# Retention outputs: a DVE block transposition and 128-byte stores in place of TensorE transposes, with the gate and the norm weight multiplied in the last stage

## The chip, the cores and the metric

One core of one Trainium2 chip runs the whole program, in one launch. The metric is the device time of that launch in microseconds. A core has TensorE (PE in the profile), VectorE (DVE), ScalarE (ACT), GpSimd (POOL), and SyncE (SP), which here issues nearly all transfers; 16 DMA engines move the data.

## What is computed

One layer of a hybrid decoder for 1024 prompt tokens and 8 x 4 sample tokens (1056 columns, NT). The part that matters is the output of the retention branch, four heads of width 512:

```python
def retention_out(o, rg, gn_w):
    mu = jnp.mean(o, axis=-1, keepdims=True)
    var = jnp.mean(jnp.square(o - mu), axis=-1, keepdims=True)
    on = ((o - mu) * lax.rsqrt(var + EPS)).reshape(b, s, RET_VW).astype(rg.dtype)
    return on * gn_w * jax.nn.silu(rg)
...
h_ret = retention_out(ret_o, rg, ret_gn_w) @ w_down_ret
h_mla = (mla_o * jax.nn.silu(mg)) @ w_down_mla
merged = jax.nn.sigmoid(ga) * h_ret + jax.nn.sigmoid(gb) * h_mla
x = x + merged @ w_out
```

Retention itself goes in chunks of 128 tokens: masked scores q k times v within the chunk, q times the state S for what came before, and S = decay x S + (decayed k) v at the end.

## The kernel before

Every fp32 product is made of three matmuls over operands split into a high and a low part (`mac`, `gemm`; names end in h and l, so vnh and vnl are the values' parts, smh and sml the scores', knh and knl the keys', Sth and Stl the state's, qch and qcl the queries'). The high part is a cast, mostly on ACT or POOL, the low part a subtraction on DVE (`lo_of`, L199).

The work runs in stages: projections woven with attention over the sample's cached pages; retention, head after head; MLA attention of the prompt; then the last stage, which multiplies by w_down_mla (eight products, M), by w_down_ret (two halves of eight), by w_out, and adds the embedding term.

The order of instructions on each engine is not the order of the code alone. Stages are generators that yield costs; `woven` interleaves several of them by these costs, and a scheduler with priorities then fixes each engine's queue. Each engine works through its queue in order, and SP does too: a transfer that waits holds up those behind it.

One head of retention is `prompt_chunks`. `front(c)` computes scores (ac<-q,k), transposes k through PSUM (tr<-k) and splits both; `values_of` projects the values of the next chunk (mm<-wv,x: 24 matmuls, spread through the chunk as filler); `back(c)` makes the output po of the chunk (vn x sm, then St x qc), the two halves m = 0, 1 of the state update (vn x kn into PSUM, then S on DVE, its parts Sth on POOL and Stl on DVE), and calls `group_norm`: BATCH_NORM_STATS, a few small steps on DVE and POOL, and on ACT the normalised rows on, 128 tokens x 512.

The last stage needs these outputs with channels on partitions. `gate_out` does that: four TensorE transposes of 128x128 into PSUM (L866), four DVE products with the norm weight gnw and the SiLU gate (L868), which `gate_in` loaded into g before the chunk (L860), and one store of 256 KB to goD (L870). It is called for 8 chunks and once for the 32 sample rows of each head: 36 calls. Those of the sample rows of heads 0 to 2 are put off (list `late`) into the next head's first chunk. Between two heads `sample_state` updates the sample's states (products vst x kx, stored to out_ret_sample) while the next head's q, k and values are projected (mm<-x,w).

In the last stage `gated` loads a 128 x 1056 tile of goD (gl), `split_gated` splits it into gh and gl, and `gate` loads the merge gates. The pool w4 has three slots.

Of the kernel before, what the change touches and what calls it, by code (L numbers as in the profile page):

```python
# [9 lines left out]
F32 = mybir.dt.float32  # L10
# [4 lines left out]
ALU = mybir.AluOpType  # L15
# [4 lines left out]
P = 128  # L20
D = 1024
SEQ = 1024
NB = 8
NS = 4
NR = NB * NS
NT = SEQ + NR
# [4 lines left out]
HR = 4  # L31
DK = 256
DV = 512
# [128 lines left out]
def decode_step(ctx: ExitStack, tc: tile.TileContext, A: dict, O: dict):  # L162
    nc = tc.nc
    pe, act, dve, pool, sp = nc.tensor, nc.scalar, nc.vector, nc.gpsimd, nc.sync
# [3 lines left out]
    dram = ctx.enter_context(tc.tile_pool(name="scratch", bufs=1, space=DRAM))  # L168
# [23 lines left out]
    def b32(ap):  # L192
        return ap.bitcast(F32)
# [4 lines left out]
    def lo_of(out, src, hi):  # L198
        dve.tensor_tensor(out=out, in0=src, in1=b32(hi), op=ALU.subtract)  # L199
# [16 lines left out]
    gaD = [dram.tile([P, NT], F32, tag=f"ga{f}", name=f"ga{f}") for f in range(8)]  # L216
    gbD = [dram.tile([P, NT], F32, tag=f"gb{f}", name=f"gb{f}") for f in range(8)]
    mgD = [dram.tile([P, NT], F32, tag=f"mg{f}", name=f"mg{f}") for f in range(8)]
    gtD, goD = ([dram.tile([P, 4, NT], F32, tag=f"{n}{h}", name=f"{n}{h}") for h in range(HR)] for n in ("gt", "go"))
    latD = dram.tile([P, 5, SEQ], F32, tag="latD", name="latD")  # L220
    xTD = dram.tile([P, 8, NT], F32, tag="xTD", name="xTD")
    pTD = dram.tile([P, 2, NT], F32, tag="pTD", name="pTD")
# [558 lines left out]
    p4 = ph.enter_context(tc.tile_pool(name="p4", bufs=1))  # L781
# [11 lines left out]
    late = []  # L793
# [61 lines left out]
        act.activation(on[:n], po, AF.Identity, bias=nb[:n], scale=s[:n])  # L855
        return on

    def gate_in(h, n, cols):
        g = p4.tile([P, 4, P], F32, tag="g", name="g", bufs=3)[:, :, :n]
        sp.dma_start(g, gtD[h][:, :, cols])  # L860
        return g

    def gate_out(h, on, n, cols, g):
        pt = tr()
        for f in range(4):
            pe.transpose(pt[:, f * P:f * P + n], on[:n, f * P:(f + 1) * P], ident[:n, :n])  # L866
        for f in range(4):
            dve.scalar_tensor_tensor(out=g[:, f, :], in0=pt[:, f * P:f * P + n], scalar=gnw[:, 4 * h + f:4 * h + f + 1],  # L868
                                     in1=g[:, f, :], op0=ALU.mult, op1=ALU.mult)
        sp.dma_start(goD[h][:, :, cols], g)  # L870

    def pair(name, w, bufs, rows_=P):
        return tuple(p4.tile([rows_, w], F32R, tag=name + s, name=name + s, bufs=bufs) for s in "hl")

    def prompt_chunks(h, X):
        q, k = X["q"], X["k"]
        V = {}
        gC = float(np.exp(P * lg[h]))
        S = p4.tile([P, 2 * DV], F32, tag="S", name="S", bufs=1)
        T = {}  # L880
        kd = C("kd", h, 1)

        def front(c):

            sl = slice(c * P, (c + 1) * P)
            pss = ac()
            for m in range(2):
                pe.matmul(pss[:, :P], k[m][:, sl], q[m][:, sl], start=m == 0, stop=m == 1)
            smh, sml = pair("sm", P, 2)
            sm = p4.tile([P, P], F32, tag="smr", name="smr", bufs=1)  # L890
            dve.tensor_tensor(out=sm, in0=pss[:, :P], in1=C("maskT", h, P), op=ALU.mult)
            act.copy(smh, sm)
            lo_of(sml, sm, smh)
            pt = tr()
            for m in range(2):
                pe.transpose(pt[:, m * P:(m + 1) * P], k[m][:, sl], ident)
            kh, kl = pair("kn", DK, 2)
            act.activation(kh, pt[:, :DK], AF.Copy, scale=kd)
            dve.scalar_tensor_tensor(out=kl, in0=pt[:, :DK], scalar=kd, in1=b32(kh), op0=ALU.mult, op1=ALU.subtract)
            return smh, sml, kh, kl  # L900

        def back(c, parts):
            sl = slice(c * P, (c + 1) * P)
            smh, sml, kh, kl = parts
            vh, vl = V.pop(c)
            if c:
                qh, ql = pair("qc", DK, 1)
                for m in range(2):
                    ms = slice(m * P, (m + 1) * P)
                    hi_pool(qh[:, ms], q[m][:, sl])  # L910
                    lo_of(ql[:, ms], q[m][:, sl], qh[:, ms])
            g = gate_in(h, P, sl)
            po = ac()
            mac(po, (smh, sml), (vh, vl), True, c == 0)
            yield 0.65
            for m in range(2 if c else 0):
                Sh, Sl = T["S"]
                ms, vs = slice(m * P, (m + 1) * P), slice(m * DV, (m + 1) * DV)
                mac(po, (qh[:, ms], ql[:, ms]), (Sh[:, vs], Sl[:, vs]), False, m == 1)
                yield 0.65  # L920
            for m in range(2):
                ms, vs = slice(m * P, (m + 1) * P), slice(m * DV, (m + 1) * DV)
                pS = ac()
                mac(pS, (kh[:, ms], kl[:, ms]), (vh, vl), True, True)
                if c:
                    dve.scalar_tensor_tensor(out=S[:, vs], in0=S[:, vs], scalar=gC, in1=pS, op0=ALU.mult, op1=ALU.add)
                else:
                    act.copy(S[:, vs], pS)
                yield 0.65
            if c < 7:  # L930
                Sh, Sl = T["S"] = tuple(p4.tile([P, 2 * DV], F32R, tag="st", name=f"St{n}", bufs=4) for n in "hl")
                for m in range(2):
                    vs = slice(m * DV, (m + 1) * DV)
                    hi_pool(Sh[:, vs], S[:, vs])
                    lo_of(Sl[:, vs], S[:, vs], Sh[:, vs])
            on = group_norm(po, P, C("qd", h, 1), C("qd2", h, 1))
            yield None
            gate_out(h, on, P, sl, g)
            yield 0.43

        def ahead(u):

            for cost in u:
                if cost is None:
                    return
                yield cost

        parts = front(0)
        yield 1.0
        yield from values_of(0, X, V)  # L950
        while late:
            gate_out(*late.pop())
        due = iter(())
        for c in range(8):
            if c == 7:
                X["st"] = [states(h, 0, 0)]
            u = back(c, parts)
            if c < 7:
                parts = front(c + 1)
                yield 1.0  # L960
                yield from woven((chain(due, ahead(u)), 3.9), (values_of(c + 1, X, V), 5.5))
                due = u
        yield None
        yield from due
# [14 lines left out]
    def sample_state(h, X):  # L979
# [3 lines left out]
        sl = slice(SEQ, NT)  # L983
# [3 lines left out]
        pt = tr()  # L987
# [25 lines left out]
        pt = tr()  # L1013
# [10 lines left out]
            dve.tensor_scalar(kxs[i], kt, C("seq2", i, 1), None, op0=ALU.mult)  # L1024
        yield 1.0
        px = ac()
        g = gate_in(h, NR, sl)
# [27 lines left out]
        on = group_norm(po[:NR], NR, C("qdS", h, 1, NR), C("qd2S", h, 1, NR))  # L1055
        yield 1.0
        if h + 1 < HR:
            late.append((h, on, NR, sl, g))
        else:
            gate_out(h, on, NR, sl, g)  # L1060
            yield 0.5

    def head_in(h, X):
        return woven((head_qk(h, X), 42.3), (head_w(h, X), 8.0))
# [26 lines left out]
    ot = slots(mph.enter_context(tc.tile_pool(name="mla", bufs=1, side="right")), "ot", HM)  # L1091
# [12 lines left out]
    def split(raw, hi, lo):  # L1104
        act.copy(hi, raw)
        lo_of(lo, raw, hi)
        return hi, lo
# [286 lines left out]
    xs_, w4 = slots(pz, "x", 23), slots(pz, "w4", 3)  # L1394
    hi_by[0] = act.copy

    def gated(f, pl):
        lo = pl("gl")
        sp.dma_start(b32(lo), goD[f // 4][:, f % 4, :])
        return lo  # L1400

    def split_gated(hi, lo):

        for j in range(3):
            sl = slice(j * TH, (j + 1) * TH)
            split(b32(lo)[:, sl], hi[:, sl], lo[:, sl])
        return hi, lo

    def load_gated(f, pl):
        lo = gated(f, pl)  # L1410
        return split_gated(pl("gh"), lo)

    def gate(src, f):
        t = w4("gate", dt=F32)
# [26 lines left out]
    gx[7] = split_gated(xr_("gh"), gx[7])  # L1441
    merged, nxt = [], []
    for half in range(2):
        for f in range(8):
# [17 lines left out]
        gx = nxt  # L1462
# [18 lines left out]
    for f in range(8):  # L1481
# [3 lines left out]
        hi, lo = xr_("x1h"), xr_("x1l")  # L1485
# [130 lines left out]
```

## Time and profile before

| | |
|---|---|
| median of 3 runs | 2175.15 us (2174.05 to 2175.59) |
| profiled execution | 2167.49 us |
| span of the profiled execution | 2165.7 us |
| TensorE busy | 2125.3 us, 98% |
| DVE / ACT / POOL busy | 1249.4 / 726.9 / 326.4 us |
| granted TensorE clock, mean | 0.998 |
| retention | about 745 to 1358 us of the span |
| w_down_mla, w_down_ret | about 1661 to 1754, 1754 to 1941 us |

The profiled execution is one run; it lies 7.7 us below the median of the others. A row of a timeline names the start, the duration, the engine, the line, and what is written from what. Matmuls overlap in the pipeline, so the time that one takes from TensorE is read from start to start. L numbers of this profile are those of the kernel before; in the changed kernel the lines of the retention stage have other numbers.

### The profile page before, as it was taken

To read this page: it belongs to the slowest core of one execution; us is meant where nothing else is said; L and a number is where in the kernel's file an instruction comes from. 1 tells how busy PE (TensorE), PEld (TensorE's weight loads), DVE (VectorE), ACT (ScalarE), POOL (GpSimd) and SP (SyncE) were. 2 spreads that over 40 slices of the span, in tenths; PEclk is the share of its full clock that TensorE was granted. 3 is DMA by queue.
4 is the path that set the end of the run, shared out by engine and by line. 5 is a ranking of instruction groups with operands and counts; after the bars stand their busy time and mean duration, and the time that the engine had idled before them with its cause. 6 is when DMAs were issued, how large, how long until landed. Compare 5 with 4: busy or idle time off the path is not lost.

```text
span 2165.7 us, 38482 instructions
## 1 busy us (share of the span) xinstructions
PE 2125.3 (98%) x15314; PEld 1854.5 (86%) x15314; DVE 1249.4 (58%) x2799; ACT 726.9 (34%) x1535; POOL 326.4 (15%) x519
## 2 busy tenths in 40 slices
PE   8999999999999999999999999899998999999998
PEld 7988777777777898888888787788888999999998
DVE  5524565565655447666666764777777353444465
ACT  6412222433423322222222211454556342222243
POOL 2210111111100022222222220122221000000022
PEclk9999999999999999999999999999999999999999
DMA  8557666566565321533613517110112453234243
GB/s 231 147 160 256 226 208 232 186 250 231 194 237 181 109 59 49 184 111 94 204 45 119 176 54 260 44 37 12 38 56 72 141 186 99 88 91 125 78 143 117
DMA packets 264356, 299.71 MB, mean 138 GB/s; under 512 B 26544, under 2 KB 221744, under 8 KB 260080
## 3 DMA queue, kind: packets, MB, share of 16 engines
q1 hardware_dynamic: 254960, 213.36, 31.8%
q0 software_dynamic: 9216, 83.89, 10.3%
q8 instruction: 120, 1.97, 0.4%
q14 instruction: 60, 0.49, 0.1%
HBM read 233.03 MB, written 64.17 MB: 137 GB/s over the span
## 4 chain that ended last, share of the span: by engine, by line
PE 41%; DVE 4%; issue 3%; DMA 1%; POOL 1%; ACT 1%; ACTq 0%; POOLq 0%; DVEq 0%
PE mm L266 10%; PE mm L267 10%; PE mm L268 10%; PE mm L1315 2%; PE ac L266 1%; PE ac L267 1%; PE ac L268 1%; PE tr L1301 1%; DMA out_ret_sample_dram<-st 1%; PE ac L1258 1%; PE ac L1259 1%; PE ac L1260 1%; PE ac L1262 1%; PE ac L1261 1%; ACT pr L1276 1%
## 5 line engine op out<-in xcount | busy, mean ns | idle before, releaser
L266 PE MATMUL mm<-xh,wh 128*128 128x352 f32 x1344 | 456.4, 340 | 0.8 <-ACT wh L247 0.6
L267 PE MATMUL mm<-xl,wh 128*128 128x352 f32 x1344 | 435.7, 324 | 0.0
L268 PE MATMUL mm<-xh,wl 128*128 128x352 f32 x1344 | 435.1, 324 | 0.1
L266 PEld LDWEIGHTS mm<-xh,wh 128*128 128x128 f32 x1344 | 252.7, 188 | 91.5 <-issue 78.9
L267 PEld LDWEIGHTS mm<-xl,wh 128*128 128x128 f32 x1344 | 253.9, 189 | 3.3 <-issue 1.0
L268 PEld LDWEIGHTS mm<-xh,wl 128*128 128x128 f32 x1344 | 253.6, 189 | 1.1 <-issue 0.6
L199 DVE TENSOR_TENSOR wl<-wr,wh 128x512 fp32r<-128x512 f32 (+2 forms) x251 | 175.0, 709 | 131.4 <-ACT wh L247 108.0
L247 ACT CAST wh<-wr 128x512 fp32r<-128x512 f32 x216 | 129.7, 618 | 303.3 <-PE mm L267 221.9
L662 DVE STREAM_TRANSPOSE kt<-craw 128x512 f32<-128x512 f32 x256 | 160.8, 681 | 84.4 <-PE sc L666 80.1
L421 ACT ACTIVATE gev<-mm 128x352 f32<-128x352 f32 x120 | 55.5, 463 | 239.3 <-PE mm L268 149.5
L268 PE MATMUL mm<-gh,wl 128*128 128x352 f32 x384 | 124.3, 324 | 0.0
L268 PE MATMUL mm<-mh,wl 128*128 128x352 f32 x384 | 124.3, 324 | 0.0
L266 PE MATMUL mm<-mh,wh 128*128 128x352 f32 x384 | 124.3, 324 | 0.0
L266 PE MATMUL mm<-gh,wh 128*128 128x352 f32 x384 | 124.3, 324 | 0.0
L267 PE MATMUL mm<-ml,wh 128*128 128x352 f32 x384 | 124.2, 324 | 0.0
L267 PE MATMUL mm<-gl,wh 128*128 128x352 f32 x384 | 124.1, 323 | 0.0
L266 PE MATMUL mm<-wv,xh 128*128 128x512 f32 x256 | 103.0, 402 | 0.0
L855 ACT ACTIVATE on<-ac,gb,gs 128x512 f32<-128x512 f32 (+1 forms) x36 | 28.0, 777 | 218.1 <-DVE gb L853 218.0
L267 PE MATMUL mm<-wv,xh 128*128 128x512 f32 x256 | 100.9, 394 | 0.0
L268 PE MATMUL mm<-wv,xl 128*128 128x512 f32 x256 | 100.7, 393 | 0.0
L666 PE MATMUL sc<-kt,q 32*32 32x512 f32 x2560 | 94.8, 600 | 0.1
L1546 POOL TENSOR_TENSOR xr<-x1h,x1l 128x352 f32<-128x352 f32 x24 | 27.0, 1146 | 389.4 <-DVE pT L199 311.1
(389 smaller groups left out, 4563.6 us busy)
## 6 DMA issues: line engine op xcount, KB each, us to landing
wr<-in_w_in_dram SPq DMA_DIRECT2D x144, 256.0 KB, 3.0
st<-in_state_ret_dram SPq DMA_DIRECT2D x32, 512.0 KB, 4.4
out_ret_sample_dram<-st SPq DMA_DIRECT2D x32, 512.0 KB, 4.0
wr<-in_w_ple_gate_dram SPq DMA_DIRECT2D x48, 256.0 KB, 2.8
gt<-gev SPq DMA_DIRECT2D x48, 176.0 KB, 3.5
gl<-go SPq DMA_DIRECT2D x16, 528.0 KB, 5.2
gate<-ga SPq DMA_DIRECT2D x16, 528.0 KB, 3.5
g<-gt SPq DMA_DIRECT2D x32, 256.0 KB, 3.1
```

The costliest lines, as they stand in the source:

```text
L199: dve.tensor_tensor(out=out, in0=src, in1=b32(hi), op=ALU.subtract)
L247: hi_by[0](hi, raw)
L266: pe.matmul(out, wh, xh, start=first, stop=False)
L267: pe.matmul(out, wh, xl, start=False, stop=False)
L268: pe.matmul(out, wl, xh, start=False, stop=last)
L421: act.activation(t, ps, func)
L662: dve.transpose(kt[:, 2 * i + s].rearrange("p (n r) -> p n r", r=32), src)
L666: pe.matmul(sc[32 * v:32 * v + 32, q, :], Q["q4"][qs_, j + v // 2, 2 * (g % 2) + v % 2, :], kt[qs_, v, :], start=n == 0, stop=n == NJ // 2 ...
L855: act.activation(on[:n], po, AF.Identity, bias=nb[:n], scale=s[:n])
L1258: pe.matmul(o, qh[:, qs], kh[:, ks], start=True, stop=False)
L1315: pe.matmul(po[:, :256], v[a][w], t[:, x, 256 * a:256 * a + 256], start=j + a + part == 0, stop=False, skip_group_check=True)
L1546: pool.tensor_tensor(out=xr, in0=b32(x1[f][0][:, sl]), in1=b32(x1[f][1][:, sl]), op=ALU.add)
```

## The change

`gate_in` and `gate_out` go. `turn_out` takes their place: one DVE instruction transposes each 32x32 block of on in place (L861 of the changed kernel, ot<-on), and four stores of 32 partitions each (L863) put the blocks where they belong: each store has 512 pieces of 32 tokens, 128 bytes, 64 KB in all. goD becomes 16 blocks x 32 channels x tokens per head. The gate and the norm weight are now multiplied in the last stage: `gated` loads gt too, into a slot of w4, and `split_gated` multiplies before it splits (three products of 128x352 for each of 16 tiles). Two yields, of 0.43 after a chunk's output and 0.5 after the last head's sample rows, go too, and with them the weaving shifts.

In numbers: 144 TensorE transposes, 144 DVE products of 128x128, 36 loads and 36 stores go; 36 DVE transpositions, 132 stores, 16 loads of 528 KB and 48 DVE products of 128x352 come.

```diff
-    gtD, goD = ([dram.tile([P, 4, NT], F32, tag=f"{n}{h}", name=f"{n}{h}") for h in range(HR)] for n in ("gt", "go"))
+    gtD = [dram.tile([P, 4, NT], F32, tag=f"gt{h}", name=f"gt{h}") for h in range(HR)]
+    goD = [dram.tile([DV // 32, 32, NT], F32, tag=f"go{h}", name=f"go{h}") for h in range(HR)]
...
-    def gate_in(h, n, cols):
...
-    def gate_out(h, on, n, cols, g):
...
+    def turn_out(h, on, n, t0):
+        st = p4.tile([P, DV // 32, 32], F32, tag="g", name="ot", bufs=3)
+        dve.transpose(st[:n], on[:n].rearrange("p (b r) -> p b r", r=32))
+        for a in range(0, n, 32):
+            sp.dma_start(goD[h][:, :, t0 + a:t0 + a + 32].rearrange("b i t -> i b t"), st[a:a + 32])
...
             on = group_norm(po, P, C("qd", h, 1), C("qd2", h, 1))
             yield None
-            gate_out(h, on, P, sl, g)
-            yield 0.43
+            turn_out(h, on, P, c * P)
...
         if h + 1 < HR:
-            late.append((h, on, NR, sl, g))
+            late.append((h, on, NR, SEQ))
         else:
-            gate_out(h, on, NR, sl, g)
-            yield 0.5
+            turn_out(h, on, NR, SEQ)
...
     def gated(f, pl):
         lo = pl("gl")
-        sp.dma_start(b32(lo), goD[f // 4][:, f % 4, :])
-        return lo
+        sp.dma_start(b32(lo), goD[f // 4][4 * (f % 4):4 * (f % 4) + 4].rearrange("b i t -> (b i) t"))
+        gt = w4("gt", dt=F32)
+        sp.dma_start(gt, gtD[f // 4][:, f % 4, :])
+        return f, lo, gt
...
-            split(b32(lo)[:, sl], hi[:, sl], lo[:, sl])
+            dve.scalar_tensor_tensor(out=gt[:, sl], in0=b32(lo)[:, sl], scalar=gnw[:, f:f + 1], in1=gt[:, sl], op0=ALU.mult, op1=ALU.mult)
+            split(gt[:, sl], hi[:, sl], lo[:, sl])
```

DVE's queue in one chunk of a head's middle, from the state update of m = 0 on, before:

```order
L926 SCALAR_TENSOR_TENSOR S<-S,ac 128x512
L851 TENSOR_TENSOR gs<-gr,cst 128x1
L853 SCALAR_TENSOR_TENSOR gb<-mv,gs 128x1
L199 TENSOR_TENSOR Stl<-S,Sth 128x512
L926 SCALAR_TENSOR_TENSOR S<-S,ac 128x512
L891 TENSOR_TENSOR smr<-ac,cst 128x128
L199 TENSOR_TENSOR vnl<-mm,vnh 128x512
L199 TENSOR_TENSOR Stl<-S,Sth 128x512
L199 TENSOR_TENSOR sml<-smr,smh 128x128
L899 SCALAR_TENSOR_TENSOR knl<-tr,cst,knh 128x256
L868 SCALAR_TENSOR_TENSOR g<-tr,gnw,g 128x128 x4
```

and in the changed kernel:

```order
L918 SCALAR_TENSOR_TENSOR S<-S,ac 128x512
L852 TENSOR_TENSOR gs<-gr,cst 128x1
L854 SCALAR_TENSOR_TENSOR gb<-mv,gs 128x1
L199 TENSOR_TENSOR Stl<-S,Sth 128x512
L861 STREAM_TRANSPOSE ot<-on 128x512
L918 SCALAR_TENSOR_TENSOR S<-S,ac 128x512
L199 TENSOR_TENSOR Stl<-S,Sth 128x512
L199 TENSOR_TENSOR vnl<-mm,vnh 128x512
L884 TENSOR_TENSOR smr<-ac,cst 128x128
L892 SCALAR_TENSOR_TENSOR knl<-tr,cst,knh 128x256
L199 TENSOR_TENSOR sml<-smr,smh 128x128
```

The products g stood at the chunk's end; the transposition stands in the middle, ahead of the update and split of the state's second half, and vnl and smr, which stood ahead of the second Stl, now stand behind it.

TensorE's queue at the same place, from the scores of the next chunk on, before:

```order
L888 MATMUL ac<-q_8114,k_8350 128x128
L888 MATMUL ac<-q_8115,k_8351 128x128
L896 MATMUL tr<-cst,k_8350 128x128
L896 MATMUL tr<-cst,k_8351 128x128
L866 MATMUL tr<-cst,on 128x128 x4
L266 MATMUL mm<-wv,xh_113 128x512
L267 MATMUL mm<-wv,xh_113 128x512
L268 MATMUL mm<-wv,xl_114 128x512
L266 MATMUL ac<-vnh,smh 128x512
L267 MATMUL ac<-vnl,smh 128x512
L268 MATMUL ac<-vnh,sml 128x512
```

and in the changed kernel:

```order
L881 MATMUL ac<-q_8114,k_8350 128x128
L881 MATMUL ac<-q_8115,k_8351 128x128
L889 MATMUL tr<-cst,k_8350 128x128
L889 MATMUL tr<-cst,k_8351 128x128
L267 MATMUL ac<-vnh,smh 128x512
L267 MATMUL mm<-wv,xh_113 128x512
L268 MATMUL mm<-wv,xh_113 128x512
L269 MATMUL mm<-wv,xl_114 128x512
L267 MATMUL mm<-wv,xh_115 128x512
L268 MATMUL mm<-wv,xh_115 128x512
L268 MATMUL ac<-vnl,smh 128x512
L269 MATMUL ac<-vnh,sml 128x512
```

With the transposes of on gone, vnh x smh stands right behind the transposes of k, and vnl x smh follows after five value products; before, four transposes and three value products stood ahead of vnh x smh, and vnl x smh came right after it.

TensorE's queue between two heads, around the turning of the sample's values (tr<-vs), before:

```order
L267 MATMUL mm<-xl_120,wh 128x352
L268 MATMUL mm<-xh_119,wl 128x352
L268 MATMUL mm<-xh_113,wl 128x352
L1014 MATMUL tr<-vs,turn 128x512
L266 MATMUL mm<-xh_121,wh 128x352
L267 MATMUL mm<-xl_122,wh 128x352
L266 MATMUL mm<-xh_115,wh 128x352
```

and in the changed kernel, from the sample values' last products (few) on:

```order
L994 MATMUL ac<-wv,few 64x512 x4
L1000 MATMUL tr<-qS,ks_9409 64x32 x2
L1025 MATMUL ac<-st,qm 32x512
L1005 MATMUL tr<-vs,turn 128x512
L1025 MATMUL ac<-st,qm 32x512 x7
L1032 MATMUL ac<-vst,kx 128x512 x2
L267 MATMUL mm<-xh_113,wh 128x352
L268 MATMUL mm<-xl_114,wh 128x352
L267 MATMUL mm<-xh_113,wh 128x352
L268 MATMUL mm<-xl_114,wh 128x352
```

The sample's steps now follow each other with the products st x qm between them; before, the next head's projections (mm<-x,w) lay between.

SP's queue between the first two heads, from the first weights of the next head behind the prompt's last state on, before:

```order
L246 DMA wr<-in_w_in_dram 128x512
L246 DMA wr<-in_w_in_dram 128x4x128 x2
L246 DMA wr<-in_w_in_dram 128x512 x2
L246 DMA wr<-in_w_in_dram 128x4x128 x2
L1046 DMA out_ret_sample_dram<-st 128x2x512 x2
L246 DMA wr<-in_w_in_dram 128x512
L975 DMA st<-in_state_ret_dram 128x2x512 x2
```

and in the changed kernel:

```order
L247 DMA wr<-in_w_in_dram 128x512
L247 DMA wr<-in_w_in_dram 128x4x128 x2
L247 DMA wr<-in_w_in_dram 128x512
L1036 DMA out_ret_sample_dram<-st 128x2x512
L247 DMA wr<-in_w_in_dram 128x512
L1036 DMA out_ret_sample_dram<-st 128x2x512
L966 DMA st<-in_state_ret_dram 128x2x512
```

The first store of sample states stands behind four weights now, where it stood behind seven.

More of the change, by code (lines that the diff above doesn't have):

```diff
@@ L856, in group_norm @@
         return on
-    def gate_in(h, n, cols):
-        g = p4.tile([P, 4, P], F32, tag="g", name="g", bufs=3)[:, :, :n]
-        sp.dma_start(g, gtD[h][:, :, cols])
-        return g
-    def gate_out(h, on, n, cols, g):
[L864 to L870, printed above, removed]
+    def turn_out(h, on, n, t0):
[3 more added lines that the diff above has]
+            sp.dma_start(goD[h][:, :, t0 + a:t0 + a + 32].rearrange("b i t -> i b t"), st[a:a + 32])
     def pair(name, w, bufs, rows_=P):
@@ L911, in back @@
                     lo_of(ql[:, ms], q[m][:, sl], qh[:, ms])
-            g = gate_in(h, P, sl)
             po = ac()
@@ L951, in prompt_chunks @@
         while late:
-            gate_out(*late.pop())
+            turn_out(*late.pop())
         due = iter(())
@@ L1026, in sample_state @@
         px = ac()
-        g = gate_in(h, NR, sl)
         out = O["ret_sample"][0].rearrange("(r i) h (m p) e -> i m h p r e", i=2, m=2)
@@ L1398, in gated, with split_gated @@
         lo = pl("gl")
-        sp.dma_start(b32(lo), goD[f // 4][:, f % 4, :])
-        return lo
-    def split_gated(hi, lo):
+        sp.dma_start(b32(lo), goD[f // 4][4 * (f % 4):4 * (f % 4) + 4].rearrange("b i t -> (b i) t"))
+        gt = w4("gt", dt=F32)
+        sp.dma_start(gt, gtD[f // 4][:, f % 4, :])
+        return f, lo, gt
+    def split_gated(hi, f, lo, gt):
         for j in range(3):
             sl = slice(j * TH, (j + 1) * TH)
-            split(b32(lo)[:, sl], hi[:, sl], lo[:, sl])
+            dve.scalar_tensor_tensor(out=gt[:, sl], in0=b32(lo)[:, sl], scalar=gnw[:, f:f + 1], in1=gt[:, sl], op0=ALU.mult, op1=ALU.mult)
+            split(gt[:, sl], hi[:, sl], lo[:, sl])
         return hi, lo
     def load_gated(f, pl):
-        lo = gated(f, pl)
-        return split_gated(pl("gh"), lo)
+        raw = gated(f, pl)
+        return split_gated(pl("gh"), *raw)
     def gate(src, f):
@@ L1440, in decode_step @@
     xr_ = slots(rph.enter_context(tc.tile_pool(name="x2", bufs=1, side="right")), "x2", 17)
-    gx[7] = split_gated(xr_("gh"), gx[7])
+    gx[7] = split_gated(xr_("gh"), *gx[7])
     merged, nxt = [], []
```

## The prediction

> **What bounds the kernel now.** I read the first part of the page, then the windows by stage, then the timeline of one chunk on each engine, and last the transfers.
>
> ```profile
> span 2165.7 us, 38482 instructions
> PE 2125.3 (98%) x15314; PEld 1854.5 (86%) x15314; DVE 1249.4 (58%) x2799; ACT 726.9 (34%) x1535; POOL 326.4 (15%) x519
> ```
>
> TensorE is busy for 98% of the span. The windows below (PE, PEld, DVE, ACT, POOL busy, granted clock, DMA share) are one head's chunks, one passage to the next head, the end of retention, and the first half of w_down_ret.
>
> ```profile
> 803.00:873.00 70.00, 69.99 (x338) 57.85 (x337) 46.66 (x124) 15.23 (x30) 15.82 (x34) 1.00 0.19 50
> 873.00:945.00 72.00, 71.30 (x412) 58.90 (x411) 46.01 (x90) 18.80 (x37) 15.84 (x21) 1.00 0.59 191
> 1300.00:1360.00 60.00, 58.69 (x337) 46.06 (x335) 25.66 (x58) 10.25 (x20) 5.49 (x15) 1.00 0.72 241
> 1754.00:1847.00 93.00, 93.00 (x578) 93.00 (x577) 45.74 (x91) 27.94 (x49) 0.00 (x0) 1.00 0.43 138
> ```
>
> In the chunks TensorE never stands (69.99 of 70.00), DVE works 46.66, and the DMA engines 0.19 of the time. So only TensorE's own instructions, or a wait put in front of one, can move the end there. The gates' load and product lie under DVE's and DMA's slack already.
>
> **The transposes that go.** TensorE around one of them:
>
> ```profile
> 852.56 0.60 PE L888 MATMUL ac<-q,k 128*128 128x128 f32 x4
> 853.00 0.38 PE L896 MATMUL tr<-cst,k 128*128 128x128 f32 x2
> 853.22 0.60 PE L866 MATMUL tr<-cst,on 128*128 128x128 f32 x4
> 853.58 0.48 PE L266 MATMUL mm<-wv,xh 128*128 128x512 f32 x1
> 853.89 0.39 PE L267 MATMUL mm<-wv,xh 128*128 128x512 f32 x1
> 854.35 0.39 PE L266 MATMUL ac<-vnh,smh 128*128 128x512 f32 x1
> 854.58 0.40 PE L267 MATMUL ac<-vnl,smh 128*128 128x512 f32 x1
> ...
> 858.30 0.39 PE L268 MATMUL ac<-Sth,qcl 128*128 128x512 f32 x1
> ```
>
> Starts count, since matmuls overlap: the four transposes hold the next one up by 0.36 us (853.22 to 853.58), and that one's successor by a further 0.08 (0.31 to 853.89 against 0.23 elsewhere). That is 0.36 to 0.44 for each of 36 calls, 13 to 16 us, call it 0.40 each. If nothing else moved, the kernel would gain 14 us. The rest of this text asks what is late next.
>
> **The loop's new order.** The same chunk on the other engines:
>
> ```profile
> 848.60 0.70 DVE L843 BATCH_NORM_STATS2 st<-ac 128x6 f32<-128x512 f32 x1 [2.38 <-PE ac L268]
> 850.77 0.61 DVE L853 SCALAR_TENSOR_TENSOR gb<-mv,gs 128x1 f32<-128x1 f32 x1
> 851.41 0.69 DVE L199 TENSOR_TENSOR Stl<-S,Sth 128x512 fp32r<-128x512 f32 x1
> 852.06 0.69 DVE L926 SCALAR_TENSOR_TENSOR S<-S,ac 128x512 f32<-128x512 f32 x1
> 853.43 0.69 DVE L199 TENSOR_TENSOR vnl<-mm,vnh 128x512 fp32r<-128x512 f32 x1
> 854.04 0.68 DVE L199 TENSOR_TENSOR Stl<-S,Sth 128x512 fp32r<-128x512 f32 x1
> 858.73 0.70 DVE L843 BATCH_NORM_STATS2 st<-ac 128x6 f32<-128x512 f32 x1 [2.38 <-PE ac L268]
> 851.48 0.78 ACT L855 ACTIVATE on<-ac,gb,gs 128x512 f32<-128x512 f32 x1 [7.47 <-DVE gb L853]
> 852.81 0.59 ACT L837 CAST vnh<-mm 128x512 fp32r<-128x512 f32 x1 [0.56 <-PE mm L268]
> 852.83 0.62 POOL L196 TENSOR_SCALAR Sth<-S 128x512 fp32r<-128x512 f32 x1 [1.46 <-DVE S L926]
> L662 DVE STREAM_TRANSPOSE kt<-craw 128x512 f32<-128x512 f32 x256 | 160.8, 681 | 84.4 <-PE sc L666 80.1
> L868 DVE SCALAR_TENSOR_TENSOR g<-tr,gnw,g x144: 235/344/351, 814.2 to 1355.1; 128x128 f32<-128x128 f32 x128, 128x32 f32<-128x32 f32 x16
> ```
>
> The period is 10.13 us (848.60 to 858.73); without the transposes TensorE's own work would be 9.69.
>
> First wait. The product vnh,smh now stands right behind the transposes of k, not behind four more transposes and three value products: TensorE is there at 853.22, while the cast vnh ends at 853.40 and is seen some 0.05 later. That is 0.23 us of new idle time.
>
> Second wait, the larger. DVE's transposition costs 0.68, as the same instruction at L662 does on the same shape: less than the four products it replaces (4 x 0.34, pipelined 1.11), so DVE's total falls. But the products stood at the end of DVE's chunk, where nobody waited for them. The transposition stands in the middle, behind on, and S m1, Stl m1 and vnl are queued behind it. Counted from BATCH_NORM_STATS at 848.60: on ends at 852.26; transposition 852.32 to 853.00; S m1 from 852.96 to 853.65 (DVE starts the next 0.04 before an end, as at 852.06); POOL's Sth from 853.73 to 854.35 (0.08 behind S, as at 852.83); Stl m1 from 854.38; vnl from 855.03 to 855.72, where it ended at 854.12 before. TensorE sees it at 855.77, 7.17 behind BATCH_NORM_STATS.
>
> What TensorE has to do in that time: the last product of po starts 0.43 before BATCH_NORM_STATS (858.30 to 858.73). From there to vnl,smh it has 28 starts of 0.232 (that product, 21 more to the chunk's end, vnh,smh and five value products) and the scores and transposes of k, 0.66 (852.56 to 853.22): 7.16 us, so vnl is due 6.73 behind BATCH_NORM_STATS and comes at 7.17. That is 0.44 us for the two waits together, whatever the first is, since a later start of vnh,smh only shortens the second. 9.69 + 0.44 = 10.13: the period that is there now, set by DVE's queue and not by TensorE. The error is in the four hand-overs, about 0.1 a chunk.
>
> This holds for chunks 2 to 7 of each head (24 chunks): 0 us, with 24 x 0.1 = 2.4 either way. In chunk 1 no state update precedes, vnl is on time, and only the first wait counts: 4 x (0.40 - 0.23) = -0.7. The eight calls outside the loop (the last chunk of each head, the sample rows) lose their transposes outright: 8 x 0.40 = -3.2. And a wait for on goes with them:
>
> ```profile
>   ACT on L855: 0.9, 2
> ```
>
> -0.9 (those two waits stood ahead of the transposes L866). Retention: -4.8 us.
>
> **The passage to the next head.** The removed yields weave the sample steps closer together.
>
> ```profile
> 896.55 1.12 PE L1014 MATMUL tr<-vs,turn 64*128 64x512 f32 x2
> 901.19 1.07 PE L1035 MATMUL ac<-st,qm 128*32 128x512 f32 x8
> 897.71 0.69 DVE L1016 CAST vr<-tr 128x512 fp32r<-128x512 f32 x1 [0.42 <-PE tr L1014]
> 898.92 0.74 DVE L1017 SCALAR_TENSOR_TENSOR vst<-vr,cst,tr 128x512 fp32r<-128x512 f32 x1
> ```
>
> Before, projections stood between tr<-vs and the product of vst; now only seven st,qm do (7/8 of 1.0 us, 901.19 to the next at 902.19). vr and vst take 0.69 + 0.74 with hand-overs of about 0.1: 1.55 - 0.87 = 0.7 us of new idle time, three times: +2.1. The weights of the next projections are queued on SP behind stores of sample states, which wait for the products of vst:
>
> ```profile
> wr<-in_w_in_dram SPq DMA_DIRECT2D x144, 256.0 KB, 3.0
> out_ret_sample_dram<-st SPq DMA_DIRECT2D x32, 512.0 KB, 4.0
> go<-g SPq DMA_DIRECT2D x32, 256.0 KB, 2.5
> gl<-go SPq DMA_DIRECT2D x16, 528.0 KB, 5.2
> ...
> go<-g SPq DMA_DIRECT2D x4, 64.0 KB, 2.6
> L870 SPq DMA_DIRECT2D go<-g x36: 520/555/566, 815.4 to 1356.1; - x36
> q1 hardware_dynamic: 528, 0.07, 11.2%
> ...
> q1 hardware_dynamic: 528, 0.26, 28.1%
> ```
>
> By the order, weights that stood ahead of the first of these stores now stand behind it. A store waits for two products of a kind with S (0.69 each) behind vst, and a weight lands 3.0 after its issue; a second buffer covers some of that. 0 to 2 us a passage, I take 0.5, +1.5. At the end of retention the latent loads and the first MLA weights stand behind the last sample stores on SP: 0.5 to 2 (one landing time at most), I take +1.
>
> **The stores.** The stores of the sample rows (64.0 KB) already consist of 512 pieces of 128 bytes. They land in 2.6 us, and in a window of 4.00 us around one (947 to 951) their 528 packets took 11.2% of 16 engines, 13.6 ns a packet; the last row is 3.10 us around a store of 256 KB in 512-byte pieces (835.5 to 838.6), 26.4 ns a packet. Four such stores a chunk are 2112 packets, 1.8 us of 16 engines in 10.1, on a share of 0.19 that also loses the gate's load: hidden. SP spends 4 x 0.56 = 2.2 us a chunk on issues; it has nothing else there.
>
> **The last stage.** 16 more loads gt of 528 KB and 48 products of 128x352. The nearest row:
>
> ```profile
> 900.93 0.52 DVE L811 TENSOR_TENSOR rt<-rx,sinR 128x352 f32<-128x352 f32 x1
> ```
>
> 48 x 0.52 = 25 us of DVE, half of it in each of two stretches of 93 us, of which the quoted one holds 45.74 of its work, on operands needed a stretch later: hidden. gt shares three slots (w4) with the gates, so SP's queue may stand for a slot; by the order every weight keeps some 5 us. 0 to 3 us, I take +0.5.
>
> **Sum** against the profiled execution (2167.49): -4.8 + 2.1 + 1.5 + 1 + 0.5 = +0.3 us, no change. It lies 7.7 us (0.35%) below the median of the runs, 2175.15; I move the median by the same amount: 2175.4, say 2175. A measurement of this kernel can tell about 0.2%, 4.35 us, from no change. With the loop's 2.4 and the passages' bounds the case spans 2170 to 2180.
>
> **Rivals.**
> 1. The waits don't come in the loop (hand-overs shorter, or vnl only just on time): the 28 loop calls gain up to 0.40 too. All of it: -14.4 - 0.9 + 5.1 = -10, 2165; with no loss in the passages 2160. With half of it, 2170. For it: the chain is only 0.44 us too long, and vnh alone would cost 0.23. Against: each of its terms is a measured row and the order leaves vnl no other place. Chance 0.29.
> 2. Slower: the transposition costs more than 0.68 here. Its input comes fresh from ACT and its four readers are stores; no row shows that. Every 0.1 us lands on vnl and so on TensorE, 24 times. The bound above is what it replaces, 1.11: +0.43 x 24 = +10, 2186. At 0.2 more (+4.8) it decides. Below, at the price of one 128x128 product, 0.34, vnl would come before vnh,smh has had its own wait out: that is the half of rival 1. Against: 256 instances at 0.68. Chance 0.18.
> 3. The last stage stands: SP waits for a slot of w4 with the weights behind it; one landing of 5.2 us on four of the 16 operands is +20, one is +5. Against: only a third to a half of DVE and 0.43 of DMA are used. Chance 0.05.
> 4. The small stores jam: if a 128-byte packet cost over 75 ns, four stores would fill the 10.1 us period (2112 packets on 16 engines). The 13.6 ns above speak against it: half the time of a 512-byte packet, for a quarter of its bytes. Chance 0.01; with 150 ns, 20 us a chunk, it would be 2490. [...]
>
> **How the numbers follow.** Forecast 0.47, rivals 0.29, 0.18, 0.05, 0.01. Faster by over 0.2%: most of rival 1 and a little of the forecast's low end, 0.28. Slower: rivals 2 to 4 and a little of the high end, 0.25. Same: 0.47. The range runs from rival 1 without losses in the passages (2160) to nearly the bound of rival 2 (2185).
>
> **What would show it.** In the chunks after: period still 10.1; TensorE idle ahead of vnh,smh (about 0.2, releaser ACT) and vnl,smh (about 0.2, releaser DVE); PE busy some 0.4 less a chunk; transposition 0.68; go stores landing under 4 us. A period of 9.7 to 9.9 proves rival 1, over 10.3 rival 2; idle time over 2 us a passage, or any in the last stage, the other terms. The forecast is wrong above all if a hand-over between engines is misjudged by more than 0.15 us.

## The result, and the profile after

The changed kernel takes 2188.82 us (2184.90 to 2191.49, 5 runs), against 2175.15 on the same chip: 1.0059 times the kernel before, with an interval of 1.0045 to 1.0073. It is slower by 13.7 us, where the forecast was no change. Ratios here and below are of fast executions; one of the six of act_keep, a kernel below, took 4109.97 us where the others took 2150.59 to 2163.40, which nothing here explains, and it counts in that kernel's median but not in its ratio. The head of the changed kernel's page:

```profile
span 2183.3 us, 38244 instructions
...
PE 2132.5 (98%) x15170; PEld 1844.2 (84%) x15170; DVE 1264.5 (58%) x2739; ACT 733.0 (34%) x1535; POOL 328.0 (15%) x519
```

TensorE has 144 instructions fewer and is busy for 7 us more. To find where, I cut both spans at the BATCH_NORM_STATS of the chunks, since each chunk has one. "Passage" below means the time from that of a head's last chunk to that of the next head's chunk 1; there are three.

| stretch | before | after | difference |
|---|---|---|---|
| start to the first chunk (code not touched) | 805.97 | 811.31 | +5.3 |
| chunk 0 to 1 of the first head | 12.23 | 11.40 | -0.8 |
| chunks 1 to 7 (first head; the difference is that of all four) | 59.87 | 60.15 | +1.3 |
| passages | 83.16, 82.85, 83.56 | 86.24, 86.24, 86.25 | +9.2 |
| last chunk to the first product M (DVE, M<-mm,gate) | 367.8 | 370.75 | +2.9 |
| the last stage, from M on | 491.1 | 490.8 | -0.3 |

The first row isn't the change's: over all profiles of this case, whose code there is the same, it lies between 803.2 and 814.8. The other rows add up to 12.3, near the 13.7 of the medians. So three quarters of the loss lie in the passages. The first passage (columns as in the prediction's windows), before:

```profile
878.07:961.23 83.16, 82.46 (x464) 67.63 (x463) 51.84 (x107) 23.24 (x48) 18.34 (x25) 1.00 0.51 163
```

and after:

```profile
882.86:969.10 86.24, 83.97 (x452) 68.49 (x451) 52.98 (x98) 23.53 (x48) 18.71 (x25) 0.98 0.47 148
```

Twelve matmuls fewer, 1.5 us more of busy time, 2.3 instead of 0.7 us idle, and a mean clock of 0.98 where it was 1.00. TensorE's timeline of that passage shows all three things:

```profile
898.10 1.05 PE L1025 MATMUL ac<-st,qm 128*32 128x512 f32 x2
899.08 1.12 PE L1005 MATMUL tr<-vs,turn 64*128 64x512 f32 x2
900.13 1.92 PE L1025 MATMUL ac<-st,qm 128*32 128x512 f32 x14
901.98 0.50 PE L1032 MATMUL ac<-vst,kx 32*128 32x512 f32 x2
...
903.25 0.49 PE L1032 MATMUL tr<-vst,kx 32*128 32x512 f32 x1
903.67 0.43 PE L269 MATMUL mm<-xh,wl 128*128 128x352 f32 x1
...
918.77 0.43 PE L269 MATMUL mm<-xh,wl 128*128 128x352 f32 x1 [2.24 <-DVE wl L199]
919.25 0.50 PE L268 MATMUL mm<-xl,wh 128*128 128x352 f32 x1
919.54 0.50 PE L269 MATMUL mm<-xh,wl 128*128 128x352 f32 x1
...
922.68 0.32 PE L269 MATMUL mm<-xh,wl 128*128 128x352 f32 x1
922.84 0.32 PE L267 MATMUL mm<-xh,wh 128*128 128x352 f32 x1
```

At 918.77 TensorE has waited 2.24 us for wl, the low part of a weight that had landed late. Behind the wait, from 919.25 to 922.68, a matmul of 352 columns starts every 0.29 us instead of every 0.16 (922.68 to 922.84): 3.4 us at a granted clock of 0.52. And groups are broken. A product st,qm is placed on a 32-wide part of the array (tile_position in the kernel, 128*32 in its row) and leaves two rows in the trace (128 rows for 64 products), so the x8 of the kernel before are four products. Those four, neighbours in the queue on different parts, took 1.00 us together (901.19 to 902.19). Now one st,qm alone holds TensorE for 0.98 (898.10 to 899.08), and the seven behind tr<-vs (x14) hold it for 1.85 (900.13 to 901.98): 2.83 us for eight products, where two whole groups took 2.00.

Why the weight was late stands in SP's queue, after:

```profile
891.86 11.43 SPq L247 DMA_DIRECT2D wr<-in_w_in_dram  x4
904.14 0.38 SPq L1036 DMA_DIRECT2D out_ret_sample_dram<-st  x1
906.58 0.34 SPq L247 DMA_DIRECT2D wr<-in_w_in_dram  x1
907.39 0.38 SPq L1036 DMA_DIRECT2D out_ret_sample_dram<-st  x1
907.86 0.42 SPq L966 DMA_DIRECT2D st<-in_state_ret_dram  x1
908.37 0.75 SPq L247 DMA_DIRECT2D wr<-in_w_in_dram  x1
911.31 0.37 SPq L966 DMA_DIRECT2D st<-in_state_ret_dram  x1
912.12 6.97 SPq L247 DMA_DIRECT2D wr<-in_w_in_dram  x2
```

The first four weights take from 891.86 to 903.29, since behind the second of them SP stands for 9.4 us (892.92 to 902.35), at the end for a weight's slot. DVE frees a slot when it has made the weight's low part (in this passage, 882 to 970, SP waited 12.1 us for wv and 11.2 for wl), and here the sample's steps stand ahead of that on both engines:

```profile
896.94 0.45 ACT L801 COPY q<-mm 128x352 f32<-128x352 f32 x1 [4.97 <-PE mm L269]
897.86 0.58 ACT L997 COPY vs<-ac 64x512 f32<-64x512 f32 x1 [0.47 <-PE ac L994]
898.35 0.62 ACT L248 CAST wv<-wr 128x512 fp32r<-128x512 f32 x1
900.97 0.75 DVE L1008 SCALAR_TENSOR_TENSOR vst<-vr,cst,tr 128x512 fp32r<-128x512 f32 x1
901.63 0.69 DVE L199 TENSOR_TENSOR wv<-wr,wv 128x512 fp32r<-128x512 f32 x1
```

Behind that, from 908.37 to 919.09, only three weights are issued: SP stands first for the state's buffer (2.2 us, to 911.31) and then, ahead of the last of the three, for a slot (5.2 us). Each sample store that stands ahead of a weight passes its own wait on as well (the eight of this passage waited 8.7 us in all for st). The weight for which TensorE waits at 918.77 was issued at 912.12 and cast at 917.13, when it had landed.

In the loop things went nearly as forecast. TensorE in the first head's chunks, after:

```profile
868.38 0.38 PE L889 MATMUL tr<-cst,k 128*128 128x128 f32 x2
868.83 0.51 PE L267 MATMUL ac<-vnh,smh 128*128 128x512 f32 x1
869.18 0.40 PE L267 MATMUL mm<-wv,xh 128*128 128x512 f32 x1
...
870.10 0.40 PE L268 MATMUL mm<-wv,xh 128*128 128x512 f32 x1
870.34 0.50 PE L268 MATMUL ac<-vnl,smh 128*128 128x512 f32 x1
870.68 0.39 PE L269 MATMUL ac<-vnh,sml 128*128 128x512 f32 x1
```

and DVE there:

```profile
863.29 0.70 DVE L844 BATCH_NORM_STATS2 st<-ac 128x6 f32<-128x512 f32 x1 [2.25 <-PE ac L269]
...
866.97 0.71 DVE L861 STREAM_TRANSPOSE ot<-on 128x512 f32<-128x512 f32 x1 [0.18 <-ACT on L856]
...
869.60 0.68 DVE L199 TENSOR_TENSOR vnl<-mm,vnh 128x512 fp32r<-128x512 f32 x1
...
873.45 0.70 DVE L844 BATCH_NORM_STATS2 st<-ac 128x6 f32<-128x512 f32 x1 [2.26 <-PE ac L269]
```

The period is 10.16. Both products that were to wait begin at the forecast places: vnh,smh 0.45 behind the transposes of k, where 0.22 would do, and vnl,smh 0.06 behind vnl's end (870.28). Each lasts 0.50 to 0.51 instead of 0.39, and its successor starts 0.34 to 0.35 later instead of 0.23. At vnl,smh that 0.11 comes with the wait. Right behind the transposes of k a product's successor is late without any wait: in late_first6, a kernel below, the first product there starts 0.14 behind them and its successor 0.32 later.

### The profile page after: what moved, and what is told of

Read it like the earlier page. It is cut to its first block, busy times and chain, and to the rows that moved or that the text cites. A ratio compares the mean times of both kernels' runs of the same rounds, so it can differ in the third digit from the quotient of the medians.

```text
span 2183.3 us, 38244 instructions
## 1 busy us (share of the span) xinstructions
PE 2132.5 (98%) x15170; PEld 1844.2 (84%) x15170; DVE 1264.5 (58%) x2739; ACT 733.0 (34%) x1535; POOL 328.0 (15%) x519
## 3 DMA queue, kind: packets, MB, share of 16 engines
q0 software_dynamic: 9216, 83.89, 10.2%
## 4 chain that ended last, share of the span: by engine, by line
PE 64%; DVE 3%; ACT 2%; POOL 1%; issue 1%; DMA 0%; ACTq 0%; SPq 0%; POOLq 0%; DVEq 0%
PE mm L267 16%; PE mm L269 15%; PE mm L268 15%; PE ac L267 2%; PE ac L268 2%; PE ac L269 2%; PE mm L1304 2%; PE tr L1290 1%; PE ac L1025 1%; PE sc L667 1%; PE ac L1247 1%; PE x L698 1%; PE ac L994 1%; PE ac L1248 1%; PE ac L1249 1%
```

## The experiments

**First round: which part of the change costs?** All four are the changed kernel with one edit; the kernel before took 2167.53 on this chip.

The number of stores, one for four:

```diff
-        for a in range(0, n, 32):
-            sp.dma_start(goD[h][:, :, t0 + a:t0 + a + 32].rearrange("b i t -> i b t"), st[a:a + 32])
+        sp.dma_start(goD[h][:, t0 // 32:(t0 + n) // 32].rearrange("b a i t -> (a i) b t"), st[:n])
```

(with goD as 16 blocks x token blocks x 32 x 32, and gl loaded in four loads of 132 KB, in pieces of 128 bytes, in the last stage)

> The changed kernel with goD laid out so that one store per chunk (2048 pieces of 128 bytes) takes the place of four, and four loads per tile in the last stage; nothing else. In the order the steps between two heads stand as before again (st,qm eight in a row, projections between). Theory A (four stores per chunk on SP's queue make the planner put the sample's steps close together, which costs weights that come late, a slower clock behind that wait, and broken groups of st,qm): the passages of 86.2 us fall to about 82.5, the wait for wl (6.7 us) and the three short stretches at half clock in the retention stage go; total 12 to 14 us below the changed kernel, 2173 to 2177, level with the kernel before. Theory B (the small pieces themselves load the DMA engines): as slow as the changed kernel, 2185 to 2190, since the pieces are the same. Loop period 10.15 by both.

The passages fell to 80.35 to 80.51, so four stores on SP in place of one cost there, by their own time or by the order that comes with them: here eight weights stand ahead of the first sample store. But the whole took 2193.72, 1.0128 (1.0113 to 1.0144): the last stage, from M on, went from 490.8 to 520.7 us. Its loads of gl, and the share of the 16 engines between 1668 and 1870:

```profile
gl<-go SPq DMA_DIRECT2D x64, 132.0 KB, 4.6
...
q1 hardware_dynamic: 83961, 32.03, 69.2%
```

and TensorE's waits in the same stretch:

```profile
PE mm L267 <- ACT wh L248: 19.0, 7, 2.7
```

So 64 loads in pieces of 128 bytes, in place of 16 in long rows, are not hidden: 69.2% of the 16 engines, and TensorE waits 19.0 us for weights. Whether the pieces or the number of loads costs this, no run tells apart.

The queue of the stores:

```diff
-            sp.dma_start(goD[h][:, :, t0 + a:t0 + a + 32].rearrange("b i t -> i b t"), st[a:a + 32])
+            act.dma_start(goD[h][:, :, t0 + a:t0 + a + 32].rearrange("b i t -> i b t"), st[a:a + 32])
```

> The changed kernel with its four stores per chunk issued by ACT instead of SP; the same stores and pieces. In the order the sample's steps stand nearly as before, but one st,qm stands apart from its group. Theory A (SP's queue): the wait for wl goes, passages 83 to 84 us, total 2176 to 2180. Theory B (pieces of 128 bytes): 2185 to 2190. ACT spends about 2 us a chunk on issues that it has free, so the loop stays at 10.1 to 10.2.

2158.54, 0.9960 (0.9945 to 0.9974): faster than the kernel before, with the same 132 stores of the same pieces. Passages of 80.87, loop periods of 10.11 to 10.13. So neither the pieces nor the transposition make the passages long: the queue does, with the order that comes with it.

The transposition's place:

```diff
-        dve.transpose(st[:n], on[:n].rearrange("p (b r) -> p b r", r=32))
+        tc.keep_in_program_order(dve.transpose(st[:n], on[:n].rearrange("p (b r) -> p b r", r=32)))
```

> The changed kernel with the transposition pinned behind what was written before it on DVE, so that it stands at the end of DVE's chunk, behind vnl. Theory of the loop (DVE's queue sets the period): the second wait goes, the first (vnh, 0.23) stays: period 9.92 instead of 10.16, 24 times, -5.7 us; the passages keep their losses: 2181 to 2185. Rival (the period is set by something else, for example TensorE or the stores): 10.15 as in the changed kernel, 2188.

The loop's period fell to 10.02, not to 9.92: vnl,smh no longer waits (0.39), but vnh,smh still does, and with 0.51 it also has the 0.11 that I had not counted. The whole is slower, 2199.56, 1.0149 (1.0134 to 1.0163), since the passages grew to 94.30. TensorE's waits in the retention stage name the weights again, here up to 6.1 us each:

```profile
PE mm L267 <- ACT wh L248: 18.2, 3, 6.1
```

The yields, put back:

```diff
             turn_out(h, on, P, c * P)
+            yield 0.43
...
             turn_out(h, on, NR, SEQ)
+            yield 0.5
```

> The changed kernel with the two removed yields (0.43 and 0.5) put back. If the yields weave the passages apart, as the prediction said: passages near 83 us, 2176 to 2180. If SP's queue does it: passages 85 to 87 us with the wait for wl of about 2 us each, 2186 to 2190.

2177.47, 1.0049 (1.0036 to 1.0061). The passages stay at 85.1, 86.4 and 85.1, with waits for wl of 6.7 us in all, and in the first of them four weights still stand ahead of the first sample store. The removed yields are at most 2.2 us of the 9.2.

**Second round: the groups, and the yields alone.** The kernel before took 2168.41 here. The best version so far, with both groups of sample products pinned to the code's order:

```diff
-                if n > 1:
-                    tc.keep_in_program_order(ins)
+                tc.keep_in_program_order(ins)
...
-                pe.matmul(pd[r], kxs[i][rs, m * P:(m + 1) * P], vst[rs], start=True, stop=True, tile_position=(32 * r, 0))
+                tc.keep_in_program_order(pe.matmul(pd[r], kxs[i][rs, m * P:(m + 1) * P], vst[rs], start=True, stop=True, tile_position=(32 * r, 0)))
```

> act_store with the products st x qm and vst x kx of the sample steps pinned behind what was written before them on TensorE, so that the one st,qm that stood apart joins its group of four. If four products of different row groups run at the same time only when they stand together (the kernel before does 16 rows of st,qm in 1.0 us where the changed kernel gives 0.98 to the single one), each passage gets 0.7 to 1.0 us shorter: 80.0 where act_store has 80.87, total 2 to 3 us below act_store. If broken groups cost nothing, 80.9 and no change.

2155.24, 0.9940 (0.9917 to 0.9963). The passages are 80.84 (with a wait of 0.9 for a state's load), 79.90 and 79.90: 0.97 below act_store in the two without that wait. A broken group costs about 1 us a passage.

The same with the transposition pinned behind vnl as well:

> act_keep with the transposition pinned to the end of DVE's chunk as in late_turn. The loop takes late_turn's period of 10.03 instead of act_store's 10.12 (the second wait goes, the first and a slow restart stay): 24 x 0.09 = 2 us less than act_keep; passages as in act_keep if the pinned order keeps weights in time, 2 us or more longer if late_turn's late weights (wh) come back.

The loop's period fell to 9.70, TensorE's own work: with this order three value products stand ahead of vnh,smh, and it doesn't wait either. But the passages rose to 83.89, 84.11 and 83.68, and the whole took 2161.86, 0.9956 (0.9940 to 0.9972): 2 us a head won in the loop, and more than that given back.

The pinned groups with the stores on SP:

> The changed kernel, stores on SP, with the sample steps' products pinned as in act_keep. This splits the passage's loss of 5.9 us against one_store (86.24 to 80.35): if broken groups are 2 us of it and the late weights with the slow clock behind them 3.8, a passage falls to 84 to 84.5 as long as the wait for wl stays; if the wait for wl goes too, to 80.5.

One profile, 2183.33 us. The expectation failed: passages of 88.25 to 89.58, with two waits for wl in each where the changed kernel had one. Pinning changed the rest of the order too, so this run does not isolate the groups.

The kernel before without its two yields:

> The kernel before without the two yields. If they held the passages together: passages of 85 us or more, 2180 to 2190. If they don't matter: passages of 82 to 83.5 us, within 3 us of the kernel before.

One profile, 2163.92 us, passages of 81.3 against 83.2, while chunks 1 to 7 grew from 59.87 to 60.72. My theory that the yields had held the passages together falls here too; without them they are shorter.

**Third round: the decisive pair**, on one chip where the kernel before took 2176.19. Of 132 stores only the 16 of each head's last chunk move to ACT's queue:

```diff
-            sp.dma_start(goD[h][:, :, t0 + a:t0 + a + 32].rearrange("b i t -> i b t"), st[a:a + 32])
+            (act if 7 * P <= t0 < SEQ else sp).dma_start(goD[h][:, :, t0 + a:t0 + a + 32].rearrange("b i t -> i b t"), st[a:a + 32])
```

> The changed kernel with only the four stores of each head's last chunk issued by ACT (16 of 132); all others stay on SP. In the order seven weights stand ahead of the first store of sample states again, and the projections stand between the sample's steps; one st,qm stands apart. If the place of these few stores on SP's queue, as the planner counts it, is what spoils the passages: 81 to 82 us each, no wait for wl, no half clock there, and 13 to 18 us less than the changed kernel on the same chip. If the number of stores on SP over the whole head matters: 84 to 86 us, gain under 5 us.

and the changed kernel once more:

> The changed kernel itself, for the same chip and hour as act_last. Expected 0.4 to 0.75% above the kernel before, passages 86.2 with a wait for wl of 2.2 each and 3.41 us at half clock right behind it, as in its first profile; the stage ahead of the retention, which no part of the change touches, may lie up to 5 us away from the first profile.

2172.20 against 2187.39: 0.9987 (0.9977 to 0.9996) and 1.0051 (1.0037 to 1.0066) of the kernel before. The first passage with the 16 stores on ACT:

```profile
886.29:967.80 81.51, 81.48 (x452) 66.52 (x451) 51.44 (x98) 23.70 (x48) 18.31 (x25) 1.00 0.49 156
```

and with them on SP:

```profile
886.07:972.48 86.41, 83.94 (x452) 68.18 (x451) 52.99 (x98) 23.60 (x48) 18.67 (x25) 0.98 0.47 147
```

The same 452 matmuls; 4.9 us less, no idle time, full clock. Three passages give 14.4 of the 15.2 us. SP's queue with the stores moved away:

```profile
895.29 13.17 SPq L247 DMA_DIRECT2D wr<-in_w_in_dram  x7
912.14 1.58 SPq L1036 DMA_DIRECT2D out_ret_sample_dram<-st  x2
```

Seven weights stand ahead of the first sample store, as before the change; with the stores on SP it was four. The four issues' own time on SP does not delay a weight: they end 5.9 us behind the last chunk's BATCH_NORM_STATS, and the first weight, which waits for a slot, is issued 9.0 us behind it in both kernels. But the third is issued 13.1 us behind it with the stores on ACT, and 19.5 with them on SP. So which queue takes these 16 stores decides how the scheduler orders the sample's steps and the weights, and that order is what costs; why it orders so, I only infer (it counts SP as taken by the stores). Over the first passages of all runs, two weights stand ahead of the first sample store in late_turn (94.3 us), four in the changed kernel and yields_back (85.1 to 86.4), and seven or eight in the others (80.4 to 83.9), except keep_sp, with six and 88.3.

The repeat also shows what the half clock is worth. In its first passage a wait of 2.25 us was followed by a stretch at half clock, after which the next weight was waited for 0.20 only. In the second, with no half clock:

```profile
1068.49 0.43 PE L269 MATMUL mm<-xh,wl 128*128 128x352 f32 x1 [2.26 <-DVE wl L199]
1068.76 0.33 PE L267 MATMUL mm<-xh,wh 128*128 128x352 f32 x1
...
1073.09 0.42 PE L269 MATMUL mm<-xh,wl 128*128 128x352 f32 x1 [1.42 <-DVE wl L199]
```

The passages took 86.41 and 86.25. So here the weights' arrival sets the end; the half clock only fills time that would have been spent waiting.

**Last: can the loop's gain be kept?** act_keep with the transposition pinned late for chunks 0 to 5 alone (turn_out pins it where its last argument is true):

```diff
-            turn_out(h, on, P, c * P)
+            turn_out(h, on, P, c * P, c < 6)
```

> The kernel act_keep (stores on ACT's queue, both sample groups pinned), with the transposition pinned to its place in the code's order (behind the state's split and vnl) for chunks 0 to 5 of each head only; TensorE's and SP's queues are those of act_keep, DVE's alone differ. Theory A (the loop's wait and the passage's weights are two separate costs; what spoilt the kernel with all transpositions late was the changed order of the queues at the passage): the five periods behind chunks 1 to 5 fall from about 10.12 to 9.69 in each head, the two last periods stay at 10.1 (6 to 7 partly), the passages stay at 79.9 to 80.9; 20 x 0.43 = 8.6 us below act_keep, a ratio to the kernel before of about 0.990. Theory B (a shorter loop alone makes the weights late, because their transfers then have less time): the passages grow to 83.7 or more as in act_late_keep and the ratio stays at 0.994 to 0.996. Theory C (vnh, not the transposition, still holds the loop): periods of 10.0, as in late_turn, a gain of 2 us.

2162.02 where the kernel before took 2176.61: 0.9935 (0.9921 to 0.9949), not to be told from act_keep's 0.9940. The periods did fall to 9.68 to 9.82, and chunks 1 to 7 from 59.75 to 57.73. But the passages grew from 79.90 to 81.96: 2.02 us won and 2.06 given back. In the first passage SP's queue is that of act_keep, but TensorE's is not quite, other than expected: tr<-vs stands four projections earlier. Theory B holds in kind, though smaller than its 83.7, and that small change of order stays as a rival. TensorE's waits in retention name what is late:

```profile
PE mm L269 <- DVE wl L199: 5.0, 5, 1.3
...
PE tr L1007 <- ACT vs L999: 1.0, 3, 0.3
```

From chunk 0 of one head to chunk 0 of the next it is 139.67 to 139.69 here and 139.64 in act_keep's second head. So in these two a faster loop does not bring the next head nearer. That the next head's weights set this time is what the waits suggest; I did not test it.

## Why the prediction was wrong, point by point

- **The bound** was right: TensorE's order and waits alone moved the end.
- **The loop** (0 forecast, +1.3 measured): right in place and nearly in size. Forecast period 10.13, measured 10.16; transposition 0.68 forecast, 0.71 measured; vnl,smh 7.17 behind BATCH_NORM_STATS forecast, 7.05 measured. The two waits were thought to be worth 0.44. It was 0.34 at vnh,smh (0.45 and 0.35 from start to start, against 0.14 and 0.32 in late_first6 at the same place) and 0.11 at vnl,smh, where TensorE came just as vnl was done; that slower start the working did not have. That DVE's queue can set the period alone is seen in act_keep: there vnh,smh stands behind value products and doesn't wait, vnl,smh does, and the period is 10.11. TensorE's own work of 9.69 is what late_first6 shows when the transposition gets out of the way, so rival 1 was real, but only in another order.
- **The step that failed is "The passage to the next head"**: +3.6 was forecast for its new waits over three passages, less about 3 for the transposes and waits that go; +9.2 came. Its cause was wrong: "The removed yields weave the sample steps closer together." With the yields back the passages stay at 85 and 86; with 16 stores off SP they are 81.5. Its sizes were wrong as well. "I take 0.5" for the late weights; the wait was 2.24, and the order that comes with the stores on SP cost 4.8 a passage in all. The order had shown it, four weights ahead of the first store instead of seven, and I priced that by one landing time of which "a second buffer covers some", when each weight must also wait for a slot that DVE frees: the third weight was issued 6.4 us later than in act_last, before any sample store. And the broken groups had no price at all, about 1 us a passage.
- **The wait for vst, 0.7 a passage**, did not come. The working took the eight rows of st,qm for eight products, and so 7/8 of 1.0 us for seven. They are four products; the seven took 1.85 (900.13 to 901.98), and vst had ended at 901.72.
- **The end of retention**: +1 forecast, +2.9 measured up to M. With the 16 stores on ACT this stretch takes 368.3 us, and 370.2 in the repeat of the changed kernel, so most of it goes with the same choice of queue; through which instructions stays open.
- **The stores** were hidden, as forecast (rival 4). In one chunk (863.3 to 873.4) their packets took 15.1% of 16 engines, 1.5 us against the 1.8 worked out, and act_store is faster than the kernel before with every one of them:

```profile
q1 hardware_dynamic: 2112, 0.26, 15.1%
```

"SP spends 4 x 0.56 = 2.2 us a chunk on issues; it has nothing else there" was true even of the last chunk, where the next head's weights are queued behind them: SP is through with the stores 5.9 us behind BATCH_NORM_STATS, and the first weight waits for its slot until 9.0. What the sentence left out is that the scheduler's order of other work changes with what stands on that queue.
- **The last stage**: +0.5 forecast, -0.3 measured; the 48 products and 16 loads are hidden, and rival 3 did not come.
- **Rival 2** is out: at 0.71 the transposition is within 0.03 of the row it was read from.

A slower kernel had a chance of 0.25, but through other mechanisms, above all a dearer transposition; it was the order that went with a queue, and at 2188.82 the time lies above the range's 2185.

## What to carry to other kernels

DMA issues that move few bytes, and here cost no time themselves (SP was through with a last chunk's four 3.1 us before the first weight went), can still change the scheduler's order of everything that shares their queue: look at the order where the stages meet, not in the loop, and try the issues on another engine's queue if that has room. Here moving 16 of 132 stores was worth 15 us, and moving all of them, with the groups pinned, turned a loss of 0.6% into a gain of 0.6%. When an order shows that a load has slipped behind stores, price the whole chain of that queue (buffer, slot, landing, split), not one landing. Count products by the program and not by rows of the trace; and check that products meant to run beside each other still stand beside each other.

## What the runs showed of the hardware that I had not expected

- A wait of 2.23 to 2.26 us was followed by 3.4 us at half clock in four of the six passages of the changed kernel's two profiles and not in the other two. The length of one wait does not decide it: in the stage behind retention a wait of 2.95 us in the kernel before (1397.48) and one of 2.94 in the changed kernel (1415.91) were followed by none (granted clock 1.00 from 1397 to 1402 and from 1415 to 1420), while behind waits of 0.76, 0.85 and 0.48 (1376.81 to 1379.75) the changed kernel's clock was 0.51 from 1380.0 to 1383.4. What decides it, no run shows.
- The stores in pieces of 128 bytes showed no cost here (15.1% of the engines' time in a chunk; act_store, with all 132 of them, took 2158.54 against 2167.53); with 64 loads of such pieces the last stage took 30 us more (520.7 against 490.8, 69.2%).
- Two products that had to wait were themselves slower, and their successors started 0.11 later: 0.50 instead of 0.39, and 0.34 instead of 0.23, at vnl,smh; 0.43 instead of 0.32, and 0.27 instead of 0.16, behind the wait at 1068.49.
